# A two-block model on one core: thirteen half columns of w_in done later in the second block's mixer

## The chip, the cores and the metric

One Trainium2 chip, of which the kernel uses one core. The metric is the device time of one execution in microseconds (us), the median of several runs. The core has TensorE (PE, with its weight loads as PEld), VectorE (DVE), ScalarE (ACT), GpSimd (POOL) and SyncE (SP), each of which works through its own instructions in order, and DMA queues that SP, ACT and POOL issue to.

## The reference

Two blocks over a sequence of 512 positions of width 1024. The first (a recurrence and pooling, a convolution module, cross attention, feed-forward layers) is untouched. The second has a mixer and a mixture of experts, and the mixer is where the change lies:

```python
h = rmsnorm(x, norm1_g[l])
p = h @ w_in[l]                       # 1024 x 5504, 43 columns of 128
p_rwkv, q, k, v, gate_logits = jnp.split(p, IN_SPLITS, axis=-1)
y_a = rwkv7_bidirectional(p_rwkv, ...) @ w_o_rwkv[l]
y_b = neighbourhood_attention_2d(q, k, v, ...) @ w_o_na[l]
g_a, g_b = jnp.split(jax.nn.sigmoid(gate_logits + b_gate[l]), 2, axis=-1)
x = x + (g_a * y_a + g_b * y_b) @ w_out[l]
```

`rwkv7_bidirectional` runs, over 512 steps and in both directions, a recurrence of a 64x64 state for each of eight heads.

## The kernel before

Everything is kept transposed: a tile is 128 features by 512 positions. `w_in` (line 1251 on) is done by **columns** of 128 features, and a column is eight blocks of 128x128, one for each tile of x. Products are made in three parts, since x and the weights are split into a high and a low half: `mm3` (lines 522 to 524) issues three 128x512 matmuls for a block. Here such a matmul is called **dense**. A column is issued in two **half columns**: `begin` does the first four blocks, `col` the last four, and the generator `columns` yields after each. So a half column is 12 dense matmuls, one rounding of 512 weight columns on ScalarE (line 352) and one subtraction on VectorE (line 354, the **split**). Behind the second half comes the **eviction**: line 1284 for the columns of q, k and v of the attention (15 to 26), line 1292 and a tanh for the gates (27 to 42), and lines 1231 to 1237 for the columns that are shifted in time (0 to 14). The list `W_IN` fixes the order of the columns: after those that the recurrence needs come 17 to 26, then 14, then the gates.

The recurrence is done in chunks of 64 steps, in these stages:

- **Preparation** (`prep`, ten steps for each of the head pairs p = 0 to 3, called turns here): decays by matmuls of lines 1444 and 1448 and a scan, products of 128x512 on VectorE (lines 1451 to 1526), Gram matrices (line 1493), transposes (line 1537).
- **Inverse** (`inverse(0)` for p = 0, 1 and `inverse(1)` for p = 2, 3): 31 steps of two VectorE instructions (lines 1565 and 1568), the **recursion**, then a copy (line 1574), transfers through DRAM and back (lines 1572 to 1585, the last one fills the tile NP), and 32x32 matmuls (lines 1593 and 1603). The first is woven into turns 2 and 3, the second follows the preparation.
- **Chunks** (`chunk`): 32 of them, issued as 16 **pairs**, each a chain over TensorE, VectorE, ScalarE and GpSimd (lines 1638 to 1715). A pair is counted here from its line 1679 to that of the next.

`near` is the attention over the grid (lines 1331 to 1399), `near_out` its output product. What is woven in where is set by strings of digits, one digit for a step: `PREP` and `INVS` for the 40 steps of the preparation, `SOLVE` and `NEAR` for the 41 of the second inverse, `GATE` and `REST` for the 32 chunks. A digit is how many steps of the other generator are taken. Two lines use them before the chunks:

```python
for g, n in ((inv, INVS), (todo, PREP)):       # 1305, after each step of prep
for g, at in ((todo, SOLVE), (near, NEAR)):    # 1315, after each step of inverse(1)
```

In the chunks (line 1781) `GATE` takes half columns, `REST` steps of the attention and, when those are at an end, half columns too; after the last chunk of p = 1 whatever is left of them is taken. From the program's order and its dependences a scheduler sets the final order of the instructions on each engine, so an instruction need not stand just where its digit is.

Of the kernel before, what the change touches and what calls it, by code (L numbers as in the profile page):

```python
# [30 lines left out]
INV = 2  # L31
AHD = 2
ENDS, ENDL = (), (3, 5, 6, 7)
PREP = "1011101111000230011101111011111111211112"
INVS = "0000000001100000000022211322222321222223"
SOLVE = "10110001011011100011010101010110101010200"
NEAR = "00001000000011000001000001000100001001000"
GATE = "01111111011110110111111101210110"
REST = "11211212112112121111121311111212"
# [403 lines left out]
class Kernel:  # L443
# [758 lines left out]
    def columns(self):  # L1202
# [100 lines left out]
        for p in range(4):  # L1303
            for _ in self.prep(p, *(kept[x, p] for x in "krv")):
                for g, n in ((inv, INVS), (todo, PREP)):
                    for _ in range(int(n[at])):
# [7 lines left out]
        for n, _ in enumerate(self.inverse(1)):  # L1314
            for g, at in ((todo, SOLVE), (near, NEAR)):
                for _ in range(int(at[n])):
# [901 lines left out]
```

## Time and profile before

| | us |
|---|---|
| median of 3 runs | 2449.68 (2449.46 to 2450.52) |
| the profiled execution, its own time | 2453.04 |
| its span, first to last instruction | 2451.3 |
| preparation, line 1444 to the first line 1593 | 1594.9 to 1743.7 |
| first 32x32 matmuls, then the second inverse's recursion | to 1761.4, then to 1804.7 |
| transfers and 32x32 matmuls of the second inverse | to 1837.8 |
| chunks | 1837.8 to about 2031 |

The profile gives, for a stretch of time, how long each engine was busy in it and the clock that TensorE was granted, as a share of full speed. "Busy" for TensorE is to be read with care: matmuls are pipelined, so one starts while others still run, and the time from start to start is what one costs in a run. The turns of the preparation are taken from their first line 1444: 1594.9, 1624.0, 1661.5 and 1694.0.

### The profile page before, as it was taken

The numbers are of one execution on the slowest core, as the hardware profiler recorded it, in microseconds if no ns is written. First come the engines' busy times: TensorE is split into PE (matmuls) and PEld (weight loads), VectorE is DVE, ScalarE is ACT, GpSimd is POOL, SyncE is SP. The second block draws the span as 40 slices with busy tenths as digits, with TensorE's granted clock in tenths as the row PEclk, the third lists the DMA queues.
The fourth block names the chain that finished last, engine by engine and source line by source line (L and its number), as shares of the span: only waits on it lengthen the run. The fifth ranks groups of instructions, "written<-read, shape, count | busy, mean of one in ns | idle before, by whom it ended". The sixth has DMA issues, their size and how long they took to land. (4 is left out here: it accounts for less than half of the span.)

```text
span 2451.3 us, 34809 instructions
## 1 busy us (share of the span) xinstructions
PE 2359.5 (96%) x13357; PEld 1830.2 (75%) x13357; DVE 1403.8 (57%) x2706; ACT 938.1 (38%) x1706; POOL 359.6 (15%) x361
## 2 busy tenths in 40 slices
PE   7999999999999999999999999999999989999996
PEld 6887888888888779788888888877876666764441
DVE  7988656545455455664645455688566766531110
ACT  4666444334244235543424234465233413321110
POOL 2112102101011000101101011211002221402211
PEclk9999999999999999999999999999889999989999
DMA  4332212222223213212222232466654435479998
GB/s 179 122 131 91 88 56 102 101 89 103 91 98 111 79 68 121 87 69 95 87 102 103 86 103 86 150 157 184 181 159 133 127 99 162 138 276 353 380 380 291
DMA packets 131196, 344.53 MB, mean 141 GB/s; under 512 B 40435, under 2 KB 66834, under 8 KB 101328
## 3 DMA queue, kind: packets, MB, share of 16 engines
q1 hardware_dynamic: 122944, 327.29, 38.7%
q0 software_dynamic: 5632, 10.49, 2.4%
q10 hardware_dynamic: 2448, 4.46, 0.5%
q8 instruction: 107, 1.75, 0.3%
q14 instruction: 65, 0.53, 0.1%
HBM read 307.33 MB, written 34.87 MB: 140 GB/s over the span
## 5 line engine op out<-in xcount | busy, mean ns | idle before, releaser
L352 ACT CAST whi<-raw 128x512 fp32r<-128x512 f32 x652 | 398.4, 620 | 710.3 <-PE acc L523 602.6
L522 PE MATMUL acc<-xn,whi 128*128 128x512 f32 x1656 | 656.6, 397 | 12.6 <-ACT xn L560 7.1
L354 DVE TENSOR_TENSOR wlo<-raw,whi 128x512 fp32r<-128x512 f32 x652 | 479.9, 742 | 307.3 <-ACT whi L352 304.3
L524 PE MATMUL acc<-xn,wlo 128*128 128x512 f32 x1656 | 651.5, 394 | 2.6 <-DVE wlo L354 2.6
L523 PE MATMUL acc<-xn,whi 128*128 128x512 f32 x1656 | 650.6, 393 | 0.0
L522 PEld LDWEIGHTS acc<-xn,whi 128*128 128x128 f32 x1656 | 312.9, 189 | 82.0 <-ACT xn L560 7.1
L524 PEld LDWEIGHTS acc<-xn,wlo 128*128 128x128 f32 x1656 | 312.6, 189 | 73.0 <-issue 3.8
L523 PEld LDWEIGHTS acc<-xn,whi 128*128 128x128 f32 x1656 | 313.1, 189 | 65.8 <-issue 1.6
L522 PE MATMUL acc<-act,whi 128*128 128x512 f32 (+1 forms) x676 | 251.3, 373 | 3.0 <-DVE tmp L1814 1.7
L523 PE MATMUL acc<-act,whi 128*128 128x512 f32 (+1 forms) x676 | 251.2, 372 | 2.7 <-DVE act L558 2.7
L524 PE MATMUL acc<-act,wlo 128*128 128x512 f32 (+1 forms) x676 | 251.0, 371 | 0.0
L721 POOL TENSOR_TENSOR tmp<-tmp 128x512 f32<-128x512 f32 x48 | 74.3, 1547 | 622.9 <-DVE tmp L719 555.8
L522 PEld LDWEIGHTS acc<-act,whi 128*128 128x128 f32 x676 | 128.3, 190 | 25.6 <-DVE tmp L1814 2.2
L523 PEld LDWEIGHTS acc<-act,whi 128*128 128x128 f32 x676 | 128.7, 190 | 25.0 <-DVE act L558 3.1
L524 PEld LDWEIGHTS acc<-act,wlo 128*128 128x128 f32 x676 | 128.5, 190 | 22.2
L580 POOL TENSOR_TENSOR tmp<-tmp 128x512 f32<-128x512 f32 x56 | 80.5, 1437 | 425.6 <-ACT tmp L573 405.1
L558 DVE TENSOR_TENSOR act<-tmp,act 128x512 fp32r<-128x512 f32 x88 | 61.1, 695 | 86.6 <-ACT act L557 84.6
L557 ACT CAST act<-tmp 128x512 fp32r<-128x512 f32 x88 | 54.4, 620 | 122.4 <-POOL tmp L721 91.2
L2096 POOL DMA_INDIRECT out<-tmp,tid x32 | 50.7, 1583 | 246.7 <-ACT tmp L2095 156.8
L701 DVE SCALAR_TENSOR_TENSOR tmp<-tmp,vec 128x512 f32<-128x512 f32 x96 | 72.2, 752 | 17.0 <-ACT tmp L698 15.3
L2064 PE MATMUL acc<-raw,xn 128*64 128x512 f32 x320 | 75.8, 602 | 4.5 <-DMA raw<-wex 4.5
L684 DVE TENSOR_TENSOR x<-x,acc 128x512 f32<-128x512 f32 x80 | 52.2, 681 | 39.5 <-PE acc L524 39.5
(438 smaller groups left out, 3176.8 us busy)
## 6 DMA issues: line engine op xcount, KB each, us to landing
raw<-wst SPq DMA_DIRECT2D x162, 1024.0 KB
raw<-wex SPq DMA_DIRECT2D x56, 1024.0 KB
whi<-wex SPq DMA_DIRECT2D x56, 256.0 KB
wlo<-wex SPq DMA_DIRECT2D x56, 256.0 KB
x<-wex SPq DMA_DIRECT2D x12, 1024.0 KB
bkv<-bkv SPq DMA_DIRECT2D x32, 192.0 KB
rec<-ab SPq DMA_DIRECT2D x8, 512.0 KB
sp_gate<-tmp ACTq DMA_DIRECT2D x16, 256.0 KB
```

The costliest lines, as they stand in the source:

```text
L352: self.nc.scalar.copy(hi, raw)
L354: self.nc.vector.tensor_sub(lo, raw, hi.bitcast(F32))
L522: nc.tensor.matmul(ps, w[0], x[0], start=first, stop=False)
L523: nc.tensor.matmul(ps, w[0], x[1], start=False, stop=False)
L524: nc.tensor.matmul(ps, w[1], x[0], start=False, stop=last)
L557: nc.scalar.copy(h, src)
L558: nc.vector.tensor_sub(lo, src, h.bitcast(F32))
L580: nc.gpsimd.tensor_add(n, accs.pop(), t)
L684: self.nc.vector.tensor_add(self.x[m], self.x[m], ps)
L701: nc.vector.scalar_tensor_tensor(z, h[:, k:k + S], taps[k], y, op0=ALU.mult, op1=ALU.add)
L721: nc.gpsimd.tensor_mul(z, u, ge)
L2064: nc.tensor.matmul(pg[a], h[:, o:o + SLOTS], w[2 * k + n], start=c + k == 0, stop=c + k == 4)
```

## The change

Three of the strings get other digits; nothing else is touched.

```diff
-PREP = "1011101111000230011101111011111111211112"
+PREP = "1011100110000130011001111001101111201111"
-SOLVE = "10110001011011100011010101010110101010200"
+SOLVE = "10110001001010100010010101010100101010100"
```

(`INVS`, between the two, stays.) The digits of `PREP` add up to 36 before and 28 now, those of `SOLVE` to 22 and 17. So 13 half columns are taken later, by the digits of `GATE` and `REST`, which stay. As the columns keep their order, every later half column slides back too: columns 23 to 26 pass from the preparation into the second inverse, with column 14 behind them, and the gates from the second half of column 30 to column 36 from there into the chunks.

In the order of TensorE the dense matmuls of this region stand so:

| | before | now |
|---|---|---|
| turns 0, 1, 2, 3 of the preparation | 79, 108, 82, 96 | 84, 63, 81, 62 |
| run ahead of the first line 1593 | 84 | 63 |
| beside the second inverse's recursion | 156 | 120 |
| run ahead of the second line 1593 | 72 | 60 |
| chunk pairs 1 to 7 | 27, 21, 27, 15, 17, 26, 6 | 15, 21, 27, 19, 13, 25, 13 |
| chunk pairs 8 to 13 | 0, 0, 0, 0, 0, 0 | 24, 18, 18, 59, 31, 0 |

**VectorE, second inverse.** Four steps of the recursion, 128x255 to 128x240 (z from X and NT; then NT). Before:

```order
L1565 TENSOR_TENSOR z<-X,NT 128x255
L1292 TENSOR_TENSOR tmp<-acc,rb 128x512
L1568 TENSOR_TENSOR NT<-NT,z 128x17x15
L1339 SCALAR_TENSOR_TENSOR ab<-ab,gqk,aux 128x512
L1565 TENSOR_TENSOR z<-X,NT 128x252
L354 TENSOR_TENSOR wlo<-raw,whi 128x512
L1568 TENSOR_TENSOR NT<-NT,z 128x18x14
```

Now:

```order
L1284 TENSOR_TENSOR tmp<-acc,rb 128x8x64
L1565 TENSOR_TENSOR z<-X,NT 128x255
L1231 MEMSET tmp 128x1
L1232 MEMSET tmp 128x1
L1568 TENSOR_TENSOR NT<-NT,z 128x17x15
L354 TENSOR_TENSOR wlo<-raw,whi 128x512
L1565 TENSOR_TENSOR z<-X,NT 128x252
L1233 TENSOR_TENSOR tmp<-acc,rb 128x512
L1568 TENSOR_TENSOR NT<-NT,z 128x18x14
```

A gate's eviction (line 1292) stood there; now an attention column's (line 1284) and the shifted column 14 (lines 1231 to 1237) do.

**TensorE, chunk pair 9**, between its line 1679 and line 1359 of the attention (w, su, bt, rb, rh are tiles of the chunk). Before:

```order
L1679 MATMUL aux<-rh,gt_12735 64x64 x8
L1690 MATMUL aux<-su,bt 64x64 x8
L1702 MATMUL aux<-w_17331,su 64x64 x4
L1707 MATMUL aux<-rb,su 64x64 x4
L1702 MATMUL aux<-w_17377,su 64x64 x4
L1359 MATMUL aux<-ab 128x256 x2
```

Now:

```order
L1679 MATMUL aux<-rh,gt_12735 64x64 x8
L522 MATMUL acc<-xn,whi 128x512
L1690 MATMUL aux<-su,bt 64x64
L523 MATMUL acc<-xn,whi 128x512
L1690 MATMUL aux<-su,bt 64x64 x7
L1702 MATMUL aux<-w_17080,su 64x64 x4
L1707 MATMUL aux<-rb,su 64x64 x4
L524 MATMUL acc<-xn,wlo 128x512
```

Dense matmuls now stand between the steps of the chain.

**TensorE, from pair 11 to the next** (lines 1643, 1651 and 1655 are the next pair's first products). Before:

```order
L1389 MATMUL aux<-cst,tmp 128x128 x4
L1651 MATMUL acc<-w_18009,bkv 64x128
L1655 MATMUL acc<-w_18009,bkv 64x64
L1396 MATMUL aux<-tmp,ab 64x128 x4
L1671 MATMUL aux<-su,w_17855 64x64 x4
```

Now, the last three of 44 dense matmuls that follow line 1396 without a break, and what stands behind them:

```order
L522 MATMUL acc<-xn,whi 128x512
L523 MATMUL acc<-xn,whi 128x512
L524 MATMUL acc<-xn,wlo 128x512
L1643 MATMUL acc<-cst,bkv 128x128 x4
L1651 MATMUL acc<-w_17678,bkv 64x128 x4
```

The next pair's products stood among this pair's; now they stand behind a run of dense matmuls. A run of 27 stands in the same way between pairs 12 and 13.

## Rows read from the trace of the kernel before

**Rows 1.** The page's busy time: engine, us, share of the span, instructions.

```profile
PE 2359.5 (96%) x13357; PEld 1830.2 (75%) x13357; DVE 1403.8 (57%) x2706; ACT 938.1 (38%) x1706; POOL 359.6 (15%) x361
```

**Rows 2.** Busy time by stretches, preparation and inverses; the first row names the columns.

```profile
core 0: us, PE busy (x) PEld busy (x) DVE busy (x) ACT busy (x) POOL busy (x), PEclk, DMA share, GB/s
1594.90:1624.00 29.10, 28.98 (x187) 21.02 (x185) 26.86 (x64) 19.64 (x36) 0.78 (x1) 1.00 0.50 122
1624.00:1661.50 37.50, 37.23 (x220) 26.99 (x218) 27.38 (x52) 20.23 (x38) 9.47 (x16) 1.00 0.78 222
1661.50:1694.00 32.50, 32.31 (x211) 24.46 (x211) 31.36 (x69) 19.37 (x40) 4.91 (x8) 1.00 0.59 138
1694.00:1724.60 30.60, 30.60 (x210) 24.57 (x210) 29.31 (x68) 15.18 (x32) 0.00 (x0) 1.00 0.61 173
1724.60:1743.70 19.10, 19.10 (x86) 15.51 (x84) 5.20 (x14) 0.00 (x0) 0.00 (x0) 1.00 1.01 271
1743.70:1761.40 17.70, 17.70 (x288) 16.13 (x288) 6.78 (x11) 7.31 (x13) 4.91 (x8) 0.63 0.38 113
1761.40:1804.70 43.30, 43.30 (x215) 33.89 (x215) 40.08 (x108) 19.12 (x37) 0.00 (x0) 0.99 0.57 196
1818.60:1837.80 19.20, 16.55 (x285) 14.47 (x284) 8.04 (x16) 6.46 (x13) 2.41 (x9) 0.62 0.19 61
```

**Rows 3.** Timeline of TensorE: start, duration, line; around the second line 1593.

```profile
1809.71 0.39 PE L522 MATMUL acc<-xn,whi 128*128 128x512 f32 x1
...
1818.33 0.39 PE L524 MATMUL acc<-xn,wlo 128*128 128x512 f32 x1
1818.65 2.21 PE L1593 MATMUL aux<-NP,go 32*32 32x32 f32 x64
```

**Rows 4.** VectorE by line in the recursion, 1761 to 1805: busy, mean ns, idle.

```profile
L354 DVE TENSOR_TENSOR wlo<-raw,whi 128x512 fp32r<-128x512 f32 x18 | 12.3, 682 | 0.1
...
L1292 DVE TENSOR_TENSOR tmp<-acc,rb 128x512 f32<-128x512 f32 x7 | 4.8, 683 | 2.0 <-PE acc L524 2.0
...
L1378 DVE TENSOR_SCALAR tmp<-tmp,ri 128x256 f32<-128x256 f32 x4 | 1.2, 340 | 0.0
```

**Rows 5.** Busy time by stretches, chunk pairs 4, 6, 8, 9, 11 to 14.

```profile
1893.43:1906.22 12.79, 12.78 (x160) 9.11 (x160) 10.15 (x32) 4.56 (x15) 3.73 (x9) 1.00 0.25 74
1920.72:1936.12 15.40, 15.38 (x160) 10.52 (x159) 11.19 (x31) 6.24 (x18) 4.18 (x11) 1.00 0.37 113
1949.73:1962.19 12.46, 9.04 (x148) 6.52 (x147) 11.36 (x37) 5.15 (x18) 3.08 (x8) 1.00 0.36 104
1962.19:1972.39 10.20, 7.82 (x132) 5.72 (x132) 8.60 (x31) 2.70 (x9) 3.08 (x8) 1.00 0.23 67
1982.56:1989.36 6.80, 5.42 (x99) 4.24 (x99) 4.15 (x18) 1.88 (x6) 3.08 (x8) 1.00 0.25 67
1989.36:2001.36 12.00, 8.97 (x133) 6.45 (x131) 6.54 (x23) 1.71 (x5) 3.17 (x8) 0.84 0.53 174
2001.36:2010.09 8.73, 7.73 (x102) 5.99 (x101) 6.14 (x22) 1.16 (x4) 1.58 (x4) 0.64 0.51 169
2010.09:2019.28 9.19, 9.12 (x125) 6.26 (x124) 6.34 (x23) 0.52 (x2) 0.79 (x2) 1.00 0.21 57
```

**Rows 6.** VectorE by line in the four turns, 1594.9 to 1724.6.

```profile
L1284 DVE TENSOR_TENSOR tmp<-acc,rb 128x512 f32<-128x512 f32 x10 | 11.3, 1129 | 1.8 <-PE acc L524 1.8
...
L1235 DVE SCALAR_TENSOR_TENSOR tmp<-tmp,vec 128x512 f32<-128x512 f32 x8 | 6.0, 749 | 1.2 <-ACT tmp L1234 1.2
...
L638 DVE SCALAR_TENSOR_TENSOR tmp<-tmp 128x32 f32<-128x32 f32 (+1 forms) x4 | 0.8, 195 | 0.0
```

**Rows 7.** Timeline of VectorE and of SP's queue: copy and transfers of both inverses.

```profile
1721.63 1.13 DVE L1574 COPY N<-NT 128x1024 f32<-128x1024 f32 x1
...
1729.43 1.53 SPq L1585 DMA_DIRECT2D NP<-dm  x2
...
1804.73 0.33 SPq L1572 DMA_DIRECT2D dn<-NT  x1
...
1812.47 1.98 SPq L1585 DMA_DIRECT2D NP<-dm  x2
```

## The prediction, made before the changed kernel was run

> **What bounds the kernel now.** Only the second mixer changes, from about 1595 to 2020 us of the span, so I read the busy time of each engine by stretches there, then the order of TensorE and VectorE, then the price of single instructions. The kernel's TensorE is nearly always "busy" [rows 1], which says little, since a busy matmul may be a slow one; the stretches say more.
>
> In the *preparation* (four heads' turns, 1594.9 to 1724.6, and a tail to 1743.7) TensorE is busy for 148.2 of 148.8 us and VectorE for 114.9 of the first 129.7, that is 89% [rows 2]. The second turn is the slack one for VectorE (27.4 of 37.5 us, 73%); the third and fourth have it at 96%. So both engines are near their limit, TensorE everywhere and VectorE in three turns of four. In the tail VectorE has little to do (5.2 of 19.1 us): there TensorE alone works off a run of 84 dense matmuls before line 1593 can start. *Dense* means a 128x512 matmul of lines 522 to 524; in a run, 39 of them start between 1809.71 and 1818.33, so one costs 8.62/38 = 0.227 us [rows 3], and a half column (12 of them) 2.72 us.
>
> In the *second inverse* the recursion of lines 1565 and 1568 takes 43.3 us, VectorE busy in 40.1 of it, 93% [rows 2], waiting for TensorE in only 2.0 [rows 4].
>
> In the *chunks* a pair of chunks with 26 dense matmuls beside it takes 15.40 us, TensorE full; one with the same other work and none takes 10.20, TensorE busy in 7.82 [rows 5]. From about 1945 on there are no half columns left: that is the room the change moves work into.
>
> **The change, part by part.** By the order, 144 dense matmuls (12 half columns; the thirteenth is still issued ahead of the chunks) leave the first two stages: 96 the preparation, 48 the second inverse. At 0.227 us they are 32.7 us of TensorE. Nothing is added or dropped, so the question is what each stage does with them.
>
> *Preparation, four turns.* The dense matmuls by turn go from 79, 108, 82, 96 to 84, 63, 81, 62: 75 fewer, 17.0 us. TensorE alone would then need 129.7 - 17.0 = 112.7 us. VectorE loses seven splits (7 x 0.682 [rows 4]) and two evictions (2 x 1.13 [rows 6]), 7.1 us, and keeps 107.8; at the 96% of the third and fourth turn that is 112.3 us, at the stage's present 89% it is 121.7. So the saving lies between 8.0 and 17.0. What takes over when TensorE gets ahead is VectorE's queue, above all in the fourth turn. I take 14.0, nearer the floor since two turns already run at 96%.
>
> *Tail.* 63 dense matmuls instead of 84: 21 x 0.227 = 4.8 us. The cover holds: line 1593 needs the NP transfer, whose issue begins at 1729.43, 7.8 us after the copy of line 1574 began, and in the second inverse the time from that issue (1812.47) to line 1593 (1818.65) is at most 6.2 [rows 3, 7]. So 14.0 us after that copy began line 1593 may start, and 63 matmuls take 14.3. I take -4.8. Were the copy later against TensorE, it would be a part of that.
>
> *Second inverse, the recursion.* Here the diff misleads: fewer half columns, but other ones. Since the columns come in a fixed order, three of the attention's v columns (23 to 26) and column 14, evicted ahead of this loop before, slide into it. Between its first instruction and the copy of line 1574 VectorE has the same 17 splits as before; five evictions of line 1292 go (5 x 0.683 = 3.4 [rows 4]), three of line 1284 come (3 x 1.13 = 3.4), a shifted column comes (one product like line 1292's, two like line 1235's at 0.749, a short one: about 2.6 us) and seven short rsqrt instructions of some 0.2 us and three small attention ones (under 0.34 each) come, 2.3 us in all [rows 4, 6]. VectorE's work grows by 4.9 us. TensorE loses 36 dense matmuls here, 8.2 us. If VectorE is the bound the loop grows by up to 4.9; if TensorE is, it shrinks by 8.2. At 93% busy VectorE is much nearer to being the bound: I take +4.0, less the wait on TensorE that may go.
>
> *Behind the recursion.* 60 dense matmuls instead of 72 before the second line 1593: 2.7 us of TensorE, but the transfers from line 1572 (1804.73) to NP (1812.47) and line 1593 (1818.65) fill this time with nothing of the columns in them [rows 3, 7]. I take 0 (at most -2.7).
>
> Up to the first chunk: -14.0 - 4.8 + 4.0 + 0 = **-14.8 us**, between -7.9 and -32.7.
>
> *Chunks, pairs 1 to 7.* 133 dense matmuls for 139: -1.0.
>
> *Pairs 8 to 10.* 24, 18 and 18 where there were none, 13.6 us. TensorE is idle there for 3.4, 2.4 and (the third is like the second) 2.4 us [rows 5], so at best they cost 5.4. By the pairs that had fillers: 15 beside pair 4 cost 0.3 us (12.79 against 12.46 with the same attention work), 26 beside pair 6 cost 5.2 (15.40 against 10.20), 0.20 each. Hence pair 8 pays 0.3 + 9 x 0.20 = 2.1, pairs 9 and 10 36 x 0.20 = 7.2: **+9.3**, between 5.4 and 13.6.
>
> *Pairs 11 and 12.* 59 and 31 more, 20.4 us. Of them 44 and 27 stand in two unbroken runs between pairs, with all of the next pair's TensorE work behind them: 71 x 0.227 = 16.1 us that hide under nothing, and 19 in between. These pairs lose their overlap too: before, the next pair's products (line 1651) were issued inside the current pair; now they follow the run. Between 16.1 and 20.4; I take **+18.5**.
>
> *Clock.* Pairs 12 and 13 have a mean granted clock of 0.84 and 0.64 [rows 5], which makes 3.8 + 6.3 = 10.1 us at the lower level of 1.2 GHz, after some 50 us without dense matmuls. A pair at 2.4 GHz without attention work takes 9.19 [rows 5], so at most 12.00 + 8.73 - 2 x 9.19 = 2.4 us come back. I take **-1.5**. The Trainium skill, "TensorE: Matmul & The Clock Gate", section "HAM oscillation", says that idle TensorE falls back to half rate and that matmuls should follow one another; by it the whole 2.4 would come back here, against the 1.5 above, a change of 0.9 us in the sum. The trace agrees in part: the fall comes in the stretch without dense matmuls, but only at its end.
>
> Chunks: -1.0 + 9.3 + 18.5 - 1.5 = **+25.3 us**, between +18.1 and +33.0.
>
> Sum: -14.8 + 25.3 = **+10.5 us**. The profiled execution took 2453.0 us, of which 2451.3 are span, so it would take 2463.5. The median of the runs shown, 2449.7, is 3.4 below the profiled one, so the median comes to **2460 us**.
>
> **The rivals.** *Slower by less, or even.* The preparation reaches TensorE's floor (-17.0), and the fillers of pairs 8 to 12 find their best packing (+5.4 and +16.1): -17.0 - 4.8 + 4.0 - 1.0 + 5.4 + 16.1 - 1.5 = +1.2, about 2451 us. For it: two engines at 96% in two turns show that the order packs well. Against it: 44 matmuls in one run.
>
> *Faster, TensorE the only bound.* If VectorE never holds TensorE up before the chunks, the first two stages give back all of their 32.7 us, the chunks still cost 25.3, and the median is 2442 us. It decides from the point where the first two stages give back more than the chunks take, 25.3 us; that needs the recursion to get shorter although its VectorE work grows. For it: TensorE is all but never idle from 1594.9 to 1804.7 [rows 2]. Against it: VectorE at 93 and 96%. The Trainium skill, "Perfetto Trace Analysis", section "Optimization Strategy", says that a kernel whose most contended engine changes over time may gain by interleaving those regimes, and this change does that: by that rule this rival is the likely one. Rows 5 bear it out for TensorE's idle time, rows 2 speak against it for VectorE.
>
> *Slower still, by the clock.* The first line 1593 to 1761.4 runs at 0.63 and the time around the second at 0.62 [rows 2]: the clock falls when TensorE has only 32x32 matmuls. The recursion now has 120 dense matmuls for 156, and if it fell there for 20 us, about 40 of them would cost another 0.2 us each: +8, 2468 us. Against it: the chunk pairs of 1949 to 1982, with none at all, keep 1.00 [rows 5].
>
> *It does not do what it says.* The order shows twelve of the thirteen half columns in the chunks; this is settled.
>
> **How the numbers follow.** Forecast (slower, 2455 to 2466): 0.52. Slower still by the clock: 0.08. Even: 0.22. Faster: 0.18. A measurement of this kernel can tell some 0.2%, 4.9 us, from no change, so: faster 0.18, same 0.22, slower 0.60. The bounds of all terms together reach from -14.6 to +25.1, which they do not all do at once; the range runs from the middle of the faster case, 2443, past the clock's, to 2470, and leaves out about half of the faster case and the worst of the slow ones, less than 2 in 10.
>
> **What would show it.** Right: the first line 1593 comes 16 to 21 us earlier; the recursion takes 46 to 48 us with VectorE above 93%, and TensorE has idle time in it for the first time; pairs 8 to 10 take 13 to 15 us; the time from pair 11's to pair 13's line 1679 grows by some 18 us, with dense runs of 10 and 6 us in it. Wrong: a recursion under 42 us (TensorE was the bound), a preparation that gives back under 8 us, dense runs that overlap with VectorE's chain, or a low clock in the recursion.

## The result, and the profile after

The changed kernel takes 2470.33 us in the median (2459.53 to 2476.31, 13 runs), the kernel before beside it 2454.2 (2449.46 to 2464.5, 13 runs). The ratio is **1.0058, 95% interval 1.0044 to 1.0072**: slower, by some 14 us. The forecast was a ratio of 2460/2449.7 = 1.0042, slower, by some 10.5. The profiled execution took 2469.18 us with a span of 2467.3, 16.0 more than that of before. Executions of one kernel differ by up to 19 us, the longer ones mostly at a lower mean clock, and a profile shows one of them; those of before and after lie 1.2 us below their medians, so the two can be compared.

TensorE's busy time grew by 15 us [rows 1] although it does the same work, VectorE's is the same:

```profile
PE 2374.6 (96%) x13357; PEld 1837.9 (74%) x13357; DVE 1404.0 (57%) x2706; ACT 937.8 (38%) x1706; POOL 361.0 (15%) x361
```

Busy time by stretches after the change, with the columns of [rows 2]: four turns up to the last dense run, this run, the time from the first line 1593 to the recursion, the recursion, the time to the second line 1593, from there to line 1643; then chunk pairs 8, 9 and 11 to 14.

```profile
1597.40:1626.50 29.10, 29.00 (x183) 20.91 (x182) 27.60 (x62) 19.64 (x36) 2.30 (x4) 1.00 0.54 130
1626.50:1652.30 25.80, 24.07 (x163) 17.03 (x162) 21.37 (x38) 16.70 (x31) 5.25 (x9) 1.00 0.75 183
1652.30:1681.70 29.40, 29.28 (x188) 21.31 (x187) 25.11 (x57) 15.00 (x29) 5.00 (x9) 1.00 0.63 149
1681.70:1716.70 35.00, 31.84 (x187) 22.85 (x187) 28.95 (x63) 17.29 (x36) 2.46 (x4) 0.90 0.61 165
1716.70:1731.10 14.40, 14.01 (x62) 11.28 (x61) 8.00 (x16) 0.63 (x1) 0.00 (x0) 1.00 0.66 120
1731.10:1753.10 22.00, 21.73 (x295) 20.41 (x296) 6.23 (x14) 8.51 (x18) 4.91 (x8) 0.58 0.67 246
1753.10:1798.80 45.70, 45.50 (x232) 35.50 (x231) 42.42 (x123) 16.71 (x36) 0.00 (x0) 0.98 0.50 168
1798.80:1809.70 10.90, 3.32 (x15) 2.44 (x14) 3.05 (x4) 1.24 (x2) 0.00 (x0) 0.84 0.98 223
1809.70:1831.70 22.00, 19.25 (x285) 16.92 (x286) 6.74 (x14) 5.92 (x12) 2.48 (x9) 0.50 0.16 47
...
1938.42:1953.58 15.16, 15.07 (x169) 10.80 (x168) 11.30 (x36) 6.75 (x21) 3.31 (x9) 1.00 0.21 63
1953.58:1966.88 13.30, 12.11 (x152) 8.76 (x151) 9.90 (x32) 4.55 (x12) 3.17 (x8) 1.00 0.39 130
...
1981.26:2003.48 22.22, 21.79 (x189) 16.39 (x188) 11.02 (x30) 6.19 (x12) 1.59 (x4) 1.00 0.62 219
2003.48:2019.24 15.76, 15.29 (x168) 11.56 (x169) 11.75 (x31) 6.86 (x15) 4.22 (x10) 1.00 0.61 199
2019.24:2025.99 6.75, 6.47 (x121) 4.84 (x119) 5.93 (x23) 1.14 (x4) 3.16 (x9) 1.00 0.35 106
2025.99:2034.17 8.18, 8.12 (x113) 5.39 (x111) 6.27 (x23) 0.50 (x2) 0.39 (x1) 1.00 0.13 36
```

Timeline after: VectorE's copy that ends the first recursion, SP's transfers into NP, TensorE's first line 1593; what stands in brackets is how long an instruction waited and for what:

```profile
1721.86 1.12 DVE L1574 COPY N<-NT 128x1024 f32<-128x1024 f32 x1
...
1726.98 1.66 SPq L1585 DMA_DIRECT2D NP<-dm  x2
...
1731.11 0.37 PE L1593 MATMUL aux<-NP,go 32*32 32x32 f32 x7 [0.41 <-DMA NP<-dm]
```

What is to be seen, stage by stage (all times of the profiled executions; the preparation is taken from its first line 1444, 1596.0 before and 1597.4 after, because what lies ahead of it took 1.4 us longer though nothing changed there; [rows 2] cut the turns of before at 1594.9, 1624.0, 1661.5 and 1694.0, but their first matmuls of line 1444 start at 1596.0, 1624.1, 1659.6 and 1690.7):

| stretch | before | after | change | forecast |
|---|---|---|---|---|
| first line 1444 to the copy of line 1574 | 125.6 | 124.5 | -1.1 | |
| that copy to the first line 1593 | 22.1 | 9.2 | -12.9 | |
| both together | 147.7 | 133.7 | **-14.0** | -18.8 |
| first line 1593 to the recursion | 17.7 | 22.0 | **+4.3** | 0 |
| recursion | 43.3 | 45.7 | **+2.4** | +4.0 |
| recursion to the second line 1593 | 13.9 | 10.9 | -3.0 | 0 |
| second line 1593 to line 1643 | 19.2 | 22.0 | +2.8 | 0 |
| pairs 1 to 7 | 104.0 | 99.2 | -4.8 | -1.0 |
| pairs 8 to 10 | 32.8 | 42.8 | **+10.0** | +9.3 |
| pairs 11 to 14 | 36.7 | 52.9 | **+16.2** | +18.5 - 1.5 |

Up to line 1643 the change gives back 7.5 us (forecast 14.8), and the pairs take 21.4 more (forecast 25.3).

### The profile page after: what moved, and what is told of

It reads as the page before. It is cut to its first block, busy times and chain, and to the rows that moved or that the text cites. A ratio compares the mean times of both kernels' runs of the same rounds, so it can differ in the third digit from the quotient of the medians.

```text
span 2467.3 us, 34811 instructions
## 1 busy us (share of the span) xinstructions
PE 2374.6 (96%) x13357; PEld 1837.9 (74%) x13357; DVE 1404.0 (57%) x2706; ACT 937.8 (38%) x1706; POOL 361.0 (15%) x361
## 5 line engine op out<-in xcount | busy, mean ns | idle before, releaser
L523 PEld LDWEIGHTS acc<-act,whi 128*128 128x128 f32 x676 | 129.3, 191 | 25.3 <-DVE act L558 3.1
L524 PEld LDWEIGHTS acc<-act,wlo 128*128 128x128 f32 x676 | 129.2, 191 | 22.1
L580 POOL TENSOR_TENSOR tmp<-tmp 128x512 f32<-128x512 f32 x56 | 80.9, 1444 | 425.0 <-ACT tmp L573 404.5
## 6 DMA issues: line engine op xcount, KB each, us to landing
raw<-wex SPq DMA_DIRECT2D x56, 1024.0 KB, 16.2
```

What stands on the lines that cost most here:

```text
L523: nc.tensor.matmul(ps, w[0], x[1], start=False, stop=False)
L524: nc.tensor.matmul(ps, w[1], x[0], start=False, stop=last)
L580: nc.gpsimd.tensor_add(n, accs.pop(), t)
```

## The experiments

Each ratio is to the kernel before, run beside it.

**One string alone.** PREP alone moves eight half columns, SOLVE alone five.

```diff
-PREP = "1011101111000230011101111011111111211112"
+PREP = "1011100110000130011001111001101111201111"
```

> Only the PREP string is changed, SOLVE as before: eight half columns pass from the preparation to the chunks (by the order, 69 of the 76 dense matmuls in pairs 8 to 11, a run of 19 at pair 11). Theory L (the loss is the long unbroken runs of dense matmuls between pairs 11 and 13, 44 and 27 of them, which exist only when both strings are changed): the preparation gives back some 12 to 17 us, the recursion takes 2 to 4 more, pairs 8 to 10 pay 5 to 6 and pair 11 pays 5 to 6, so within 5 us of the kernel before, ratio 0.997 to 1.002. Theory U (every half column costs about its 2.7 us wherever it stands in the chunks, and VectorE sets the time ahead of them): 8/13 of the +14 us of the whole change, about +9, ratio 1.0035. Theory Q (the transfer into X, line 1558, which stands on SP's queue behind line 1481 here as in the changed kernel, holds up the first inverse): the first line 1565 starts 14 to 15 us after the third turn's first line 1444, not 0.4 us as before.

```diff
-SOLVE = "10110001011011100011010101010110101010200"
+SOLVE = "10110001001010100010010101010100101010100"
```

> Only the SOLVE string is changed, PREP as before: five half columns pass from the second inverse to the chunks (pairs 1 to 10 have 15, 21, 27, 19, 13, 25, 13, 24, 21, 9 dense matmuls, none in pairs 11 and 12). The columns of the recursion are those of before, so it loses splits and gate evictions, some 4 to 5 us of VectorE. Theory L (the loss of the whole change is the long runs at pairs 11 and 12): the recursion falls from 43.3 to 38 to 40 us, pairs 1 to 7 gain or lose under 3, pairs 8 to 10 pay 4 to 6 us; total -5 to +1, ratio 0.998 to 1.000. Theory U (each half column costs the chunks 2.7 us and the recursion gives nothing back): 5/13 of +14, about +5 us, ratio 1.002.

Measured: 1.0018 (1.0001 to 1.0035) for PREP alone, 0.9992 (0.9976 to 1.0007) for SOLVE alone. They add up to 1.0010; both together are 1.0058. So the last of the thirteen half columns cost far more than the first. Both ratios are within theory L's bounds, and U's 1.002 for SOLVE lies outside the measured interval; the next run shows that it is not the runs' length that makes the last ones dear. With PREP alone the first line 1593 came 132.9 us behind the first line 1444 and the recursion took 46.5 us: these two parts of the changed kernel belong to PREP. The first line 1565 came 15.0 us into the third turn, as theory Q said (before, it came 2.3 us into it, not the 0.4 of the expectation). With SOLVE alone the recursion fell by 1.0 us to 42.3 (theory L had 38 to 40), and the chunks took 48 more dense matmuls and yet 1.7 us less. The rows of SOLVE alone: recursion, the time behind it, second line 1593 to line 1643, and pairs 11 to 13.

```profile
1764.60:1806.90 42.30, 42.30 (x211) 33.01 (x210) 39.57 (x110) 19.33 (x40) 0.00 (x0) 1.00 0.56 184
1806.90:1817.80 10.90, 3.90 (x18) 2.89 (x16) 3.11 (x5) 1.24 (x2) 0.00 (x0) 0.86 0.93 226
1817.80:1839.70 21.90, 19.22 (x284) 16.87 (x284) 6.74 (x14) 5.92 (x12) 2.40 (x8) 0.50 0.15 45
1990.32:1997.36 7.04, 6.17 (x116) 4.96 (x118) 6.01 (x24) 1.86 (x6) 3.08 (x8) 1.00 0.51 156
1997.36:2003.35 5.99, 4.97 (x103) 4.04 (x99) 5.20 (x20) 1.62 (x5) 1.57 (x5) 1.00 0.74 250
2003.35:2011.20 7.85, 6.81 (x123) 5.00 (x123) 6.52 (x23) 1.26 (x4) 2.67 (x7) 1.00 0.81 257
```

Two things are read here. Pairs 11 to 13 with no dense matmul and the full clock take 20.9 us; in the kernel before the same pairs took 6.80 + 12.00 + 8.73 = 27.5, two of them at a low clock [rows 5]. The low clock is only a part of these 6.7 us. Below stand TensorE's longest wait in these pairs before, and the same pairs of two kernels that come further down and whose chunks have no dense matmul there either: the kernel before without the splits of two turns, and the change turned round.

```profile
PE acc L1651 <- DMA w<-rec: 2.6, 1, 2.6
...
1995.06:2017.61 22.55, 18.71 (x326) 14.06 (x326) 16.73 (x63) 4.78 (x14) 7.83 (x20) 0.99 0.60 184
...
1992.11:2017.57 25.46, 22.52 (x327) 17.01 (x327) 16.81 (x62) 4.74 (x14) 7.83 (x20) 0.77 0.52 161
```

In neither of the two does TensorE wait for that transfer. At a clock of 0.99 they take 22.55 us, at 0.77 2.9 more; before, the wait of 2.6 leaves some 2.4 of the 5.0 us above 22.55 for the clock. So the clock is worth 2.4 to 2.9 us here, the wait as much, and the rest of the 6.7 is not parted.

And the shorter run behind the recursion (60 matmuls for 72) saves 3.0 us and loses 2.7 again: TensorE is busy in 3.90 of 10.9 us while the transfers run, and then does its 32x32 matmuls at a mean clock of 0.50 instead of 0.62, in 21.9 us for 19.2 [rows 2].

**The runs of dense matmuls broken up.** The changed kernel, half columns taken by GATE alone.

```diff
-                other, out = chain(near, gates), self.near_out()
+                other, out = near, self.near_out()
...
-                            for _ in other:
+                            for _ in chain(near, gates):
```

> The changed kernel, with the half columns in the chunks taken by GATE alone; REST takes only the attention's steps and no half columns when these are at an end (what is left is taken at the same place as before, behind the last chunk of p = 1). Everything ahead of the chunks and pairs 1 to 10 stay; pairs 11 to 15 have 24, 11, 37, 13 and 25 dense matmuls for 59, 31, 0, 11 and 6; the runs are 8, 27 and 12 long for 44 and 27. Theory L (the long runs cost their full 0.227 us per matmul because the next pair's chain stands behind them): pairs 11 to 15 together take 5 to 10 us less than in the changed kernel, total 2460 to 2466 where the changed kernel has 2470. Theory U (fillers cost the same wherever they stand): within 2 us of the changed kernel.

Measured: 1.0057 (1.0036 to 1.0077), the changed kernel's time. Pairs 11 to 13:

```profile
1983.69:1998.15 14.46, 13.99 (x154) 9.71 (x153) 8.35 (x26) 3.49 (x8) 1.59 (x4) 1.00 0.56 169
1998.15:2008.31 10.16, 9.61 (x129) 6.66 (x128) 6.79 (x23) 1.66 (x5) 4.50 (x11) 1.00 0.62 227
2008.31:2024.51 16.20, 15.73 (x155) 11.42 (x154) 9.52 (x28) 5.00 (x11) 2.45 (x7) 1.00 0.41 139
```

Against the 20.9 us without dense matmuls, 72 of them cost 40.8 - 20.9 = 19.9 us here, 0.28 each; in the changed kernel 90 cost 44.7 - 20.9 = 23.9, 0.27 each. A part is not theirs: of the next pairs' small products (lines 1643, 1651 and 1655) more stand in these pairs than with SOLVE alone, 56 of line 1651 in the changed kernel and 48 here for 36, which by their distance from start to start is an estimated 2.4 and 1.0 us. That leaves 0.24 for a matmul in the changed kernel and 0.26 here, where the longest runs are 27 and 12 for 44 and 27. The long runs are not worse than shorter ones: theory L is wrong, U right for these pairs. Without attention beside them they leave TensorE idle for only 1 us each (SOLVE alone: 6.17 of 7.04, 4.97 of 5.99, 6.81 of 7.85), so nothing hides a filler.

**Fillers where a pair has room.** The kernel before, its twelve half columns one to a pair. Besides the two lines above:

```diff
-GATE = "01111111011110110111111101210110"
+GATE = "01010101010101010101010100000000"
```

> The kernel before, with its last twelve half columns in the chunks taken one to a pair (GATE 01 twelve times, then zeros; REST takes the attention's steps alone). Pairs 1 to 10 have 19, 8, 15, 13, 12, 12, 13, 22, 13, 12 dense matmuls for 27, 21, 27, 15, 17, 26, 6, 0, 0, 0. Theory C (a pair hides the first 10 to 12 dense matmuls in TensorE's idle time, so a filler is cheap where a pair has few and costs its 0.2 us where it has many): pairs 1 to 7 take 6 to 10 us less, pairs 8 to 10 take 2 to 5 more, and pairs 11 to 13 take 21 instead of 27.5 if the low clock goes as it did with only SOLVE changed; total 3 to 14 us faster, ratio 0.994 to 0.999. Theory U (every filler costs the same 0.2 us wherever it stands): within 2 us of the kernel before, clock apart.

Measured: **0.9961 (0.9946 to 0.9976)**, 2443.7 us: faster than both kernels. Pairs 1 to 7, 8 to 10 and 11 to 13, of this kernel:

```profile
1847.18:1935.97 88.79, 86.90 (x1119) 63.89 (x1118) 70.46 (x210) 33.59 (x113) 26.52 (x68) 1.00 0.40 124
1935.97:1976.50 40.53, 38.16 (x461) 26.63 (x460) 33.11 (x103) 15.80 (x45) 9.73 (x24) 1.00 0.38 114
1976.50:2002.84 26.34, 21.67 (x324) 16.93 (x324) 17.50 (x63) 5.34 (x15) 7.88 (x20) 0.81 0.56 169
```

and of the kernel before:

```profile
1845.77:1949.73 103.96, 102.18 (x1169) 71.42 (x1168) 75.27 (x217) 39.92 (x125) 26.92 (x67) 1.00 0.40 128
1949.73:1982.56 32.83, 24.69 (x412) 17.99 (x411) 28.57 (x97) 10.55 (x36) 9.24 (x24) 1.00 0.28 81
1982.56:2010.09 27.53, 22.12 (x327) 16.67 (x327) 16.83 (x62) 4.75 (x14) 7.83 (x20) 0.81 0.45 146
```

47 dense matmuls fewer in pairs 1 to 7 saved 15.2 us, 0.32 each; the same 47 cost 7.7 us in pairs 8 to 10, 0.16 each. Theory C has the direction right, a filler is cheaper where a pair has few, but both amounts are above what it said: the first ten or twelve of a pair are not hidden whole. The low clock stayed, so that part of it did not come.

**The change turned round.** The kernel of the last run, with four half columns more in the second inverse.

```diff
-SOLVE = "10110001011011100011010101010110101010200"
+SOLVE = "10110001011011100011110111011110111010200"
...
-GATE = "01010101010101010101010100000000"
+GATE = "01010101010101010000000000000000"
```

> The kernel before with its half columns in the chunks one to a pair, as in the run before, and the change turned round: four half columns more in the second inverse (SOLVE adds up to 26), so eight are left for the chunks. By the order 48 dense matmuls pass from pairs 8 to 10 to the recursion and the time behind it; pairs 1 to 7 stay nearly as they are. Theory D (VectorE bounds the recursion): four splits and two evictions more, 4.1 us, of which some 3 can go into its idle time: the second inverse takes 1 to 4 us more, pairs 8 to 10 take 7 to 8 less, in all 0.9930 to 0.9955 of the kernel before. Theory T (TensorE bounds the second inverse, 48 x 0.227 = 10.9 us more there): 8 to 11 more against 7 to 8 less, 0.996 to 0.998.

Measured: 0.9993 (0.9978 to 1.0008), worse than either theory. Recursion, the time behind it, and pairs 8 to 10:

```profile
1766.30:1807.90 41.60, 41.60 (x208) 32.90 (x208) 38.52 (x105) 19.14 (x37) 0.00 (x0) 0.99 0.58 203
1807.90:1831.30 23.40, 23.40 (x105) 18.61 (x103) 10.77 (x19) 7.43 (x14) 0.00 (x0) 1.00 0.78 207
...
1955.53:1992.11 36.58, 28.32 (x408) 20.60 (x409) 28.00 (x95) 11.57 (x38) 9.24 (x24) 0.86 0.25 74
```

The recursion did not grow; the second line 1593 came 23.4 us behind it for 13.9, TensorE busy throughout. That is T's mechanism: behind VectorE's chain stands TensorE's backlog. The clock fell in the chunks besides (0.86 in pairs 8 to 10, where before it was 1.00), at least in this execution: it is the longest of the kernel's twelve, 2461.58 us for a median of 2452.39.

**What bounds the recursion.** First, the 17 splits of the second inverse on GpSimd, which has nothing to do there (`low` is GpSimd during the second inverse, VectorE elsewhere; the lines that set it are not shown).

```diff
-        self.nc.vector.tensor_sub(lo, raw, hi.bitcast(F32))
+        getattr(self, 'low', self.nc.vector).tensor_sub(lo, raw, hi.bitcast(F32))
```

> The changed kernel with the 17 splits (line 354) that are issued during the second inverse done by GpSimd instead of VectorE; GpSimd has nothing else to do there. The order on TensorE differs only a little. Theory D (VectorE's queue bounds the recursion, 42.5 us of work in 45.8): 17 splits of 0.68 us leave it, so it falls by 6 to 11 us, to 35 to 40. Theory T (TensorE's 120 dense matmuls and the attention's products bound it, busy for 45.6 of 45.8 us): it falls by under 2, or grows because the splits come later.

Measured: 1.009 (1.0065 to 1.0115); the recursion fell to 42.9 us, between the theories, but started 27.3 us behind the first line 1593 for 22.0. The timeline of VectorE and GpSimd says why this does not decide (start, duration):

```profile
1771.19 0.42 DVE L1568 TENSOR_TENSOR NT<-NT,z 128x252 f32<-128x252 f32 x1
...
1771.60 3.94 POOL L354 TENSOR_TENSOR wlo<-raw,whi 128x512 fp32r<-128x512 f32 x3 [2.97 <-ACT whi L352]
1771.65 1.50 DVE L1565 TENSOR_TENSOR z<-X,NT 128x255 f32<-128x255 f32 x1
...
1773.07 2.61 DVE L1378 TENSOR_SCALAR tmp<-tmp,ri 128x256 f32<-128x256 f32 x2
```

While GpSimd subtracts, a step of 128x255 takes VectorE 1.50 us instead of 0.42, and two of line 1378 take 2.61 instead of 0.68 [rows 4]. So the splits were left out instead, the high half standing in for the low one (`whole` is set during the second inverse; the lines that set it are not shown):

```diff
-        lo = pool.tile([P, n], F32R, name="wlo", bufs=bufs)
-        self.nc.vector.tensor_sub(lo, raw, hi.bitcast(F32))
+        lo = hi if getattr(self, "whole", None) else pool.tile([P, n], F32R, name="wlo", bufs=bufs)
+        if lo is not hi: self.nc.vector.tensor_sub(lo, raw, hi.bitcast(F32))
```

> The changed kernel without the 17 splits (line 354) of the second inverse: the high half of the weights is used in place of the low one there, so that VectorE's work is left out and nothing is put on GpSimd. TensorE has the same matmuls in nearly the same order. Theory D (VectorE's queue bounds the recursion): 17 x 0.68 = 11.6 us of the 42.5 us of VectorE's work go, and the recursion falls from 45.8 to 34 to 40 us, with VectorE still the busier engine against what TensorE needs. Theory T (TensorE's work beside it bounds the recursion as much): it falls by under 3 us, to 43 or more, and VectorE's busy share falls below 75%.

Measured: 1.0031 (1.0015 to 1.0047), some 7 us less than the changed kernel. Recursion, the time to the second line 1593, and from there to line 1643:

```profile
1756.40:1788.50 32.10, 32.04 (x176) 24.64 (x174) 30.71 (x92) 12.76 (x27) 0.00 (x0) 1.00 0.60 209
1788.50:1802.30 13.80, 13.80 (x62) 11.15 (x61) 7.30 (x14) 4.12 (x10) 0.00 (x0) 1.00 1.00 248
1802.30:1821.60 19.30, 16.47 (x285) 14.46 (x285) 8.04 (x16) 6.53 (x13) 2.44 (x9) 0.62 0.18 52
```

32.1 us for 45.7, VectorE busy in 96%: theory D, and more of it than was expected. VectorE's queue bounds the recursion, although TensorE shows as busy all the time. Of the 13.6 us 2.9 were lost again behind it, where TensorE's run comes last, and 2.7 came back behind that (19.3 us for 22.0, at a clock of 0.62 for 0.50).

**What bounds the preparation.** Four half columns, from the first half of PREP alone:

```diff
-PREP = "1011101111000230011101111011111111211112"
+PREP = "1011100110000130011001111011111111211112"
```

> The kernel before with four half columns fewer in the preparation (the first half of PREP as changed, its second half as before; SOLVE as before). By the order 48 dense matmuls leave the stretch ahead of the first line 1593 and stand in chunk pairs 7 to 9 (17, 21, 17 there for 6, 0, 0). Theory S (slack: before the change TensorE's backlog set the first line 1593, 22.1 us behind the copy of line 1574, while in the changed kernel 9.2 were enough; up to 12.9 us can be given back, at 0.227 us per matmul, and nothing beyond): from the first turn's first line 1444 to the first line 1593 it is 147.7 - 10.9 = 136.8 us, and the copy stays at 125.6, within 1.5. Theory P (each half column gives back the share that eight gave with only PREP changed, 14.8/8 = 1.85): 140.3 us. The later columns slide into the second inverse, which costs 2 to 6 us there, and the chunks change by -2 to +5. Total by S: 2 to 9 us faster than the kernel before, ratio 0.9965 to 0.999; by P: 1.000 to 1.002.

Measured: 1.0007 (0.9992 to 1.0021). The first line 1593 came 141.8 us behind the first line 1444, -5.8: less than both theories said. Busy time in the 12 us up to a fall of the clock in the fourth turn, in the 13 us of this fall, and from the copy to line 1593:

```profile
1683.00:1695.00 12.00, 12.00 (x58) 8.96 (x58) 11.12 (x27) 1.54 (x3) 1.54 (x3) 1.00 0.73 241
1695.00:1708.00 13.00, 13.00 (x47) 8.85 (x44) 10.43 (x22) 9.05 (x18) 0.00 (x0) 0.61 0.36 105
...
1724.30:1739.30 15.00, 15.00 (x68) 12.13 (x67) 5.15 (x8) 0.00 (x0) 0.00 (x0) 1.00 0.92 236
```

A mean clock of 0.61 over 13.0 us is 2 x 0.39 x 13.0 = 10.1 us at 1.2 GHz instead of 2.4, which loses 5.1 us of TensorE; theory S's -10.9 and this make -5.8. So S is right if the fall is set against it, and that is worked out, not measured: this profile is of the longest of the kernel's twelve executions (2460.91 us for a median of 2456.56), and how many of them have this fall is not shown. Before, the clock is 1.00 in all four turns [rows 2]. In the changed kernel it is 0.90 in the fourth; its 12 us up to the fall:

```profile
1690.00:1702.00 12.00, 10.53 (x76) 7.70 (x75) 12.00 (x27) 7.89 (x16) 0.00 (x0) 1.00 0.41 102
```

There TensorE has gaps ahead of the fall. With four half columns less the profile shows it busy without a gap, in fewer matmuls: 58 in 12.0 us, where the last of the four stretches of before has 210 in 30.6 [rows 2].

To part the two chains that meet at line 1593, the splits of the third and fourth turn were left out in the same way (`whole` is set during these turns), in the kernel before and in the changed one:

> The kernel before without the splits (line 354) of the third and fourth turn: the high half of the weights is used in place of the low one there, so that some 15 to 20 VectorE instructions of 0.68 us are left out. By the order 36 dense matmuls of the second inverse come ahead of the first line 1593, in a run of 120 for 84. Theory S (two chains meet at the first line 1593: VectorE's, which ends in the copy of line 1574 and the transfers behind it, and TensorE's backlog, which comes last by 12.9 us in the kernel before): the copy comes 6 to 13 us earlier than 125.6 us behind the first line 1444, and the first line 1593 does not come earlier; it comes 5 to 9 us later than 147.6, by the 36 more dense matmuls. Theory V (VectorE alone bounds the preparation): the first line 1593 comes earlier with the copy.

> The changed kernel without the splits (line 354) of the third and fourth turn: the high half of the weights is used in place of the low one there, some 16 VectorE instructions of 0.68 us less. By the order 48 dense matmuls of the second inverse come ahead of the first line 1593, in a run of 96 for 65. Theory S (in the changed kernel VectorE's chain to the copy of line 1574 and TensorE's backlog meet nearly together at the first line 1593): the copy comes 4 to 9 us earlier than 124.5 us behind the first line 1444; the first line 1593, now behind TensorE alone, comes up to 10.9 us later than 133.7, more than 15 us behind the copy. Theory W (the copy in the changed kernel waits for the third and fourth turn's products through ScalarE and the transfers, not for VectorE's queue, which is busy in 87% of the time): the copy comes less than 3 us earlier.

Measured: 1.0017 (1.0004 to 1.0031) and 1.0056 (1.0039 to 1.0073). Timeline of the first (its first line 1444 at 1598.6):

```profile
1714.87 1.08 DVE L1574 COPY N<-NT 128x1024 f32<-128x1024 f32 x1
...
1754.07 0.40 PE L1593 MATMUL aux<-NP,go 32*32 32x32 f32 x7
```

The copy came 116.2 us behind the first line 1444 (-9.4), line 1593 155.4 (+7.8; 36 x 0.227 = 8.2). In the second the copy came 6.4 us earlier and line 1593 2.6 later, 18.2 behind it. Theory S holds in both: VectorE's work moves the copy, TensorE's backlog sets line 1593.

**The transfer into X.** In the changed kernel the first recursion starts 5.3 us later than before although its turn starts 7.3 earlier; the transfer into X is issued by SP at 1660.40, behind line 1481, where before it was issued at 1651.09:

```profile
1659.86 0.37 SPq L1481 DMA_DIRECT2D rec<-ab  x1
1660.40 0.45 SPq L1558 DMA_DIRECT2D X<-dx  x1
```

```diff
-        nc.sync.dma_start(X, dx.rearrange("e b n s t -> (e b n) s t"))
+        (nc.sync if g else nc.scalar).dma_start(X, dx.rearrange("e b n s t -> (e b n) s t"))
```

> The changed kernel, with the transfer into X of the first inverse (line 1558) issued by ScalarE instead of SP. Chunks have the same dense matmuls as in the changed kernel. Theory Q (in the changed kernel this transfer stands on SP's queue behind line 1481, whose issue waits for VectorE's products of the third turn; it began at 1660.4 us, 10 us behind the last dx, where the kernel before issued it at 1651.1, and that is where the second turn's 11.7 us went): the first line 1565 starts 5 to 9 us earlier than 1667.2, the copy of line 1574 3 to 6 us earlier than 1721.9, the first line 1593 2 to 6 us earlier than 1731.1, and the kernel takes 2 to 6 us less than the changed one. Theory V (VectorE's amount of work sets the two turns' end whenever the recursion starts): the copy moves by under 1.5 us and the total by under 2.

Measured: 1.0059 (1.0038 to 1.0079), no gain, and no answer: on ScalarE's queue the transfer was issued at 1661.4, no earlier, the copy came 124.3 us behind the first line 1444 for 124.5, and 48 dense matmuls slid ahead of line 1593 by the order. Whether an early transfer would have brought the copy forward stays open.

## Why the prediction came out as it did

Its verdict, slower, and its form, a small gain ahead of the chunks against a larger loss in them, held. That the sum came as near as +10.5 to some +14 is in part luck: it gave back 7.3 us too much ahead of the chunks and charged 3.9 too much in them. Step by step:

- **Preparation, -18.8 against -14.0.** The step that failed is the split into turns (-14.0) and tail (-4.8). Line 1593 waits for two chains. VectorE's, up to the copy, came out almost where it was (-1.1): the fourth turn begins 84.3 us behind the first line 1444 instead of 94.6, but from there to the copy it takes 40.2 us instead of 30.9. VectorE has its own 31 steps and products to do, as the splits left out show, and it begins the steps 15.0 us into the third turn instead of 2.3; whether the transfer into X is to blame for that stays open. TensorE's backlog was 22.1 us behind the copy and could shrink to 9.2, where the transfer to NP takes over (the bracket at 1731.11); with PREP alone, GATE alone and the two runs on the recursion's splits line 1593 comes 9.3 or 9.4 us behind the copy as well. That is 12.9 us, whatever the matmuls removed were worth. The prediction put this floor at 14.0 us behind the copy; NP's issue came 5.1 us behind it, not 7.8, and line 1593 4.1 us behind the issue (1726.98 to 1731.11), not 6.2. Its sign of being right, line 1593 16 to 21 us earlier, did not come.
- **The clock in the preparation** was not in the prediction. With fewer matmuls in the turns TensorE ran at 1.2 GHz for 2 x 0.10 x 35.0 = 7.0 us of the fourth. Such a fall stands in the profiles of six of the eight kernels with the first half of PREP changed (not with the transfer into X on ScalarE's queue, nor with the changed kernel's splits left out of the turns) and in none of the five others. What it cost the changed kernel at line 1593 is not shown. The rival "by the clock" had the mechanism and the wrong place, the recursion, where the clock stayed at 0.98. The Trainium skill, "TensorE: Matmul & The Clock Gate", section "HAM oscillation", says that idle TensorE falls back to half rate; the prediction used this for the 2.4 us to be had back, and did not ask what the change itself does to the clock where it takes matmuls away. The trace agrees with the rule in part: behind the second inverse the clock fell where TensorE had stood idle (3.32 of 10.90 us busy), and ahead of the fall in the fourth turn it had gaps too (10.53 of 12.00 us busy), but with four half columns less it was busy for 12.00 of the 12.00 us ahead of its fall.
- **First line 1593 to the recursion, +4.3, forecast 0.** The same slide of the columns that the prediction followed into the recursion also brought 24 matmuls of line 646 (a column's sums of squares) into this stretch, where none were, at a low clock. In the profiles with 24 of them there the stretch takes 22.0 us or more, in those with none 14.9 to 18.3. TensorE by line there:

```profile
L1603 PE MATMUL aux<-gt,NP 32*32 32x32 f32 x128 | 6.8, 236 | 0.0
L646 PE MATMUL aux<-cst,tmp 128*128 128x2 f32 x24 | 5.6, 355 | 0.3 <-ACT nsums L1257 0.3
L1593 PE MATMUL aux<-NP,go 32*32 32x32 f32 x128 | 5.4, 207 | 0.4 <-DMA NP<-dm 0.4
```

- **Recursion, +4.0 against +2.4.** Right, though a little short of the 46 to 48 us named, and shown to be VectorE's: it did not shrink although 36 dense matmuls left it, VectorE stayed at 93%, and without the splits it fell to 32.1. That TensorE would show idle time in it did not come: a busy TensorE is a waiting one there.
- **Behind the recursion, 0 against -3.0 + 2.8.** Right in sum and wrong in the reason: before, TensorE's run came last, not the transfers; the 3.0 us saved were lost to the clock behind it (0.50 for 0.62, and the same 128 matmuls of line 1593 are busy for 7.2 us instead of 5.4).
- **Pairs 8 to 10, +9.3 against +10.0.** Right, though not all of it is the columns': before, pair 7 held 32 matmuls of line 1651, the products of two pairs, and now 16, so a set of small products, an estimated 1.7 us by their distance from start to start, moved from pairs 1 to 7 into the pairs behind.
- **Pairs 11 to 14, +17.0 against +16.2.** Right in sum by two errors. The 90 dense matmuls cost up to 23.9 us, some 21.5 without the small products, not 18.5, since the pairs without attention have next to no idle time. What they replaced was worth 6.7 us in pairs 11 to 13, not 1.5: 2.4 to 2.9 for the low clock, about as much for a wait for a transfer that the prediction did not see, and a rest. Its "at most 2.4" for the clock came out about right by luck, since pair 14, which it took for a pair without columns, has 11 dense matmuls in it before. That the runs are to blame, which the prediction took from the order, fell: in shorter runs they cost the same.
- **Pairs 1 to 7, -1.0 against -4.8.** A term mis-sized: pair 1 alone lost 12 of its 27 dense matmuls and 3.3 us (16.0 to 12.7), where a matmul costs nearer 0.3 than 0.20, and the small products of pair 8 left this stretch, an estimated 1.7 us. The six fewer in all would be 1.9 even at 0.32.

The *faster* rival needed TensorE to be the bound up to the chunks. It is, at the first line 1593, for 12.9 us; in the recursion it isn't. The rule of the Trainium skill behind that rival ("Perfetto Trace Analysis", section "Optimization Strategy", on interleaving regimes) gave no gain in this change and did in another: half columns moved from full pairs to empty ones gained 0.4%.

## What to carry to other kernels

Where two chains meet, what an engine saves counts only up to the point where the other chain comes last: measure that distance (22.1 against 9.2 us here) before adding up what is removed. Price a filler by its neighbours in the place it goes to, since the same matmul cost 0.16 us in some chunk pairs and 0.32 in others, and ask what the place it leaves does with an idle TensorE, because it may pay in clock what it saves in work. Spreading fillers evenly over pairs that have room was worth more than moving them between stages.

## What the runs showed of the hardware

- The clock fell in the fourth turn (0.90 there after the change, 0.61 over 13 us with four half columns less) where the turns had lost dense matmuls, with TensorE busy in 10.53 of the 12.00 us ahead of the first fall and in 12.00 of 12.00 ahead of the second. What let it fall in the second is not shown by these runs.
- The 32x32 matmuls from the second line 1593 to line 1643 took 19.2 and 19.3 us (clock 0.62) where TensorE was busy up to them, before and without the splits (13.80 of 13.80 us), and 21.9 to 22.0 (0.50) where it was busy in some third of the 10.9 us ahead of them. In between lies the kernel before without the splits of the turns: 21.3 us (0.53) behind 8.21 of 10.3 us.
- GpSimd holds VectorE up: an instruction with two inputs in SBUF rose from 0.42 to 1.50 us beside a GpSimd subtraction of 1.31 us. The Trainium skill, "SBUF — State Buffer", section "Who interferes with whom", says that VectorE instructions with two such inputs contend with a GpSimd instruction that reads there, and that the second to start waits for the whole of the first; the trace agrees.
